# A two-layer encoder in split fp32: output operands get buffers of their own, casts go behind the probabilities' cast, first products are reordered, a product moves from GpSimd to VectorE

## The chip, the cores and the metric

The kernel runs on one core of a Trainium2 chip. The metric is the device time of one execution in microseconds (us); the figure for a kernel is the median of its runs. Engines are called TensorE (PE in the profile), VectorE (DVE), ScalarE (ACT), GpSimd (POOL) and SyncE (SP). Every engine works through its own instructions in one fixed order, and waits at an instruction until what that needs has been signalled by another engine or by a DMA. "L648" is line 648 of the kernel before.

## The reference

Two sequences (512 and 256 tokens, 768 in all, 2048 features, fp32) pass through two layers. Layer 0 projects x to an SSM branch (a_u, a_g) and to a grouped attention branch with 8 heads and 2 key/value heads (q, k, v, b_g); layer 1 is a dilated mixture attention with 16 heads and a gate. Cut to what matters here:

```python
# layer 0
a_u, a_g, q, k, v, b_g = split(x @ even_w_in)
ya = s5(a_u); ya = ya * sigmoid(ya @ glu_w + glu_b)           # the gated linear unit
q = rmsnorm(q) * qn_g; q = rotary(q, row | col); k likewise    # cosine and sine products
yb = softmax(q @ k.T * scale) @ v
y = concat(ya * silu(a_g), yb * silu(b_g)) @ even_w_out
x = layernorm(ALPHA * x + y) * ln_g + ln_b
# layer 1
q, k, v, g = split(x @ odd_w_in)
y = (dilated_mixture(rotary(q), rotary(k), v) * silu(g)) @ odd_w_out
out = layernorm(ALPHA * x + y) * ln_g + ln_b
```

## The kernel before, in words

Every fp32 operand of a matrix product is split into a high part (a cast on ScalarE, L441 or L447, names ending in h) and a low part (the difference, on VectorE or GpSimd, L442 or L448, names ending in l). A product is then three matmuls: high by high, high by low, low by high. Activations live in `c.xh` and `c.xl`, 16 blocks of 128 features by 768 tokens; weights are loaded by SyncE (`wr`, `b`) and split into `wh`, `wl`.

The order of the work is written out by hand as a recording. Long matmul loops (`proj_f`, L536, 128x384 products into `pa`/`pb`; `proj_t`, L580, products into `pt`; `Seven.product`, L753) call `fill(c)` after each group of products. `fill` takes a function from the queue `c.q` and runs what `later(c, n, f)` has put down for n fills from now. So small pieces (transposes, attention steps, norms) are placed between groups of long products. A scheduler then orders each engine's instructions; `tc.issue_after(x)` keeps an instruction behind x on its engine, and a tile pool gives out buffers, so a tile is only written once the readers of its buffer's last use are done.

Five places matter:

- **Query blocks** (`qk_block`, `q_block`, L635 to L675). Four blocks of queries, each in three parts i. A part is copied from PSUM, normalised (`qss`, `qn`: L660 to L663, with a power on GpSimd at L662), multiplied by a sine table (four products, `qsq`, L669, VectorE) and by a cosine table (two products 128x256, `qr`<-`qn`,`qkc`, L672, GpSimd), summed (L673, VectorE) and transposed on TensorE (`ps_q`, L648) after the number of fills in `at`. The keys go the same way. For the last block `at` is (1, 2, 3).
- **Attention of layer 0** (`Attn.step`). A step issues the scores of one unit of 128 queries (`ps_sc`, L843), turns the probabilities `pp` of the unit two steps earlier (`ps_pt`, L872, split into `pth` and `ptl` by `split_ps`), and, when a sequence is complete, the values (`ps_o`, L885). Steps stand in `c.q` between the products of the last gate (`late_gate(7)`) and of the gated linear unit (L1142 on, one fill per six products). One `fill(c, 2)` stands between these two (L1141).
- **First products of layer 1** (`Seven`). Layer 1's projections are done by seven products of sums of blocks in place of eight. For the first four weight pairs n, products 0 and 3 need no sums and are done alone (`Seven.alone`, L1302 on); ScalarE copies each result to `early` (L761). The sums of activations come from VectorE (L1208), ScalarE casts them (L1216), VectorE takes the low part.
- **Gates of layer 1** (`gate_sb`, L1437). The projections come back from DRAM into a `res` tile; ScalarE takes a tanh (L1439, 128x768), VectorE the product (L1440). This happens for two heads at a time, 16 heads in all.
- **First block of the output projection** (L1485 to L1505). While the last head pair's attention steps still run, the block of 256 output columns is started: `mix_in(k)` loads head k's mixed values from DRAM into a `res` tile (three buffers, shared with queries, keys and gates of the last heads), and splits it into `c.xh[k]`, `c.xl[k]`. It runs three blocks ahead of the products. `residual1` applies the norm's scale and offset to the residual `res0` in two passes on GpSimd (L1350, 128x1536), each with a row tile `lrow` fetched by GpSimd's queue.

## Time and profile before

| | us |
|---|---|
| median of 3 runs | 2634.8 (2634.49 to 2635.05) |
| the profiled execution's own time | 2632.97 |
| its span | 2631.2 |

| engine | busy, us | share of the span | instructions |
|---|---|---|---|
| TensorE (PE) | 2541.3 | 97% | 15632 |
| VectorE (DVE) | 1787.2 | 68% | 3516 |
| ScalarE (ACT) | 1050.0 | 40% | 2102 |
| GpSimd (POOL) | 772.5 | 29% | 641 |

About 1.8 us of the profiled execution lie around its span. The mean granted clock of TensorE is 0.986 of full speed. A view that lists waits names, for each instruction that stood idle, the engine and the tile that released it; a timeline row gives the start, the length, the engine, the line, the instruction with output and inputs, and in brackets the idle time before it. Long rows of equal products are grouped by "xN".

### The profile page before, as it was taken

Reading aid. Unit: us, or ns where it says so; the run is one execution under the profiler, and the core shown is the slowest. Engines: PE = TensorE matmul, PEld = TensorE weight load, DVE = VectorE, ACT = ScalarE, POOL = GpSimd, SP = SyncE. Lnnn points to the kernel's source line nnn. Section 1 sums busy time; section 2 is a strip of 40 time slices with the busy share of each in tenths; the row PEclk is TensorE's granted clock in tenths of the full one; section 3 lists DMA queues with packets and bytes.
Section 4 is the critical chain, followed back from the end, with each engine's and each line's share of the span. In section 5 each row is a group of like instructions: output and inputs, shape, how many; then the busy total and the mean of one; then the engine's idle time right before and its main releaser. Section 6 shows DMA issues by size and latency. Waiting matters only on the chain.

```text
span 2631.2 us, 41939 instructions
## 1 busy us (share of the span) xinstructions
PE 2541.3 (97%) x15632; PEld 2432.2 (92%) x15632; DVE 1787.2 (68%) x3516; ACT 1050.0 (40%) x2102; POOL 772.5 (29%) x641
## 2 busy tenths in 40 slices
PE   7999999999999999998999999999999999989996
PEld 7999999999988998888999999999999999988886
DVE  6488998878445542238866666778788878763437
ACT  4322233222237731117433333456555656651111
POOL 2555666645564420004000000012212212244404
PEclk9999999999999999999999999999999999989998
DMA  5433333332354462125443444454544454456222
GB/s 154 124 88 99 96 98 97 102 88 71 110 150 141 142 207 64 64 89 165 138 131 124 129 126 127 137 117 111 119 115 109 112 117 113 101 163 196 77 74 106
DMA packets 353451, 308.59 MB, mean 117 GB/s; under 512 B 60384, under 2 KB 305120, under 8 KB 352352
## 3 DMA queue, kind: packets, MB, share of 16 engines
q1 hardware_dynamic: 333200, 265.83, 33.3%
q0 software_dynamic: 10688, 36.71, 6.9%
q10 hardware_dynamic: 9360, 3.38, 0.7%
q8 instruction: 123, 2.02, 0.3%
q14 instruction: 80, 0.66, 0.1%
HBM read 232.10 MB, written 67.44 MB: 114 GB/s over the span
## 4 chain that ended last, share of the span: by engine, by line
PE 70%; DVE 16%; DMA 4%; issue 3%; POOL 2%; ACT 1%; SPq 0%; DVEq 0%; POOLq 0%; ACTq 0%
PE pt L580 23%; PE ps_y L753 12%; PE ps_z L753 8%; PE ps_x L753 8%; PE pa L536 4%; PE pb L536 4%; PE ps_o L885 3%; PE ps_sc L843 2%; DMA res<-pd 2%; PE ps_pt L872 2%; DVE wl L442 1%; DVE tmpv L227 1%; DVE xs L370 1%; PE ps_y L410 1%; DVE sc_sw L369 1%
## 5 line engine op out<-in xcount | busy, mean ns | idle before, releaser
L441 ACT CAST wh<-wr 128x512 fp32r<-128x512 f32 x348 | 216.3, 622 | 715.3 <-PE pt L580 391.5
L580 PE MATMUL pt<-wh,xh 128*128 128x256 f32 (+1 forms) x1392 | 458.8, 330 | 0.9 <-DVE z L898 0.8
L580 PE MATMUL pt<-wl,xh 128*128 128x256 f32 (+1 forms) x1392 | 456.1, 328 | 0.0
L580 PE MATMUL pt<-wh,xl 128*128 128x256 f32 (+1 forms) x1392 | 455.9, 327 | 0.0
L442 POOL TENSOR_TENSOR wl<-wr,wh 128x512 fp32r<-128x512 f32 x176 | 245.1, 1398 | 532.7 <-ACT wh L441 470.0
L442 DVE TENSOR_TENSOR wl<-wr,wh 128x512 fp32r<-128x512 f32 x172 | 145.8, 849 | 257.0 <-ACT wh L441 256.4
L580 PEld LDWEIGHTS pt<-wh,xh 128*128 128x128 f32 x1392 | 265.8, 191 | 25.0 <-issue 2.5
L580 PEld LDWEIGHTS pt<-wl,xh 128*128 128x128 f32 x1392 | 265.8, 191 | 22.3
L580 PEld LDWEIGHTS pt<-wh,xl 128*128 128x128 f32 x1392 | 265.5, 191 | 22.3
L753 PE MATMUL ps_y<-xh,wh 128*128 128x384 f32 x768 | 260.0, 339 | 0.0
L753 PE MATMUL ps_y<-xl,wh 128*128 128x384 f32 x768 | 257.1, 335 | 0.9 <-DVE xl L1208 0.9
L753 PE MATMUL ps_y<-xh,wl 128*128 128x384 f32 x768 | 257.0, 335 | 0.0
L441 ACT CAST wh<-b 128x512 fp32r<-128x512 f32 x248 | 151.6, 619 | 184.4 <-PE ps_z L753 91.5
L442 DVE TENSOR_TENSOR wl<-b,wh 128x512 fp32r<-128x512 f32 x248 | 170.2, 688 | 38.4 <-ACT wh L441 38.2
L753 PE MATMUL ps_x<-xh,wh 128*128 128x384 f32 x512 | 176.1, 344 | 7.5 <-ACT early L761 6.1
L753 PE MATMUL ps_z<-xh,wh 128*128 128x384 f32 x512 | 174.1, 340 | 0.0
L753 PE MATMUL ps_x<-xh,wl 128*128 128x384 f32 x512 | 172.0, 336 | 0.0
L753 PE MATMUL ps_x<-xl,wh 128*128 128x384 f32 x512 | 171.9, 336 | 0.0
L753 PE MATMUL ps_z<-xh,wl 128*128 128x384 f32 x512 | 171.4, 335 | 0.0
L753 PE MATMUL ps_z<-xl,wh 128*128 128x384 f32 x512 | 171.1, 334 | 0.0
L536 PE MATMUL pa<-xh,wh 128*128 128x384 f32 x448 | 158.3, 354 | 4.4 <-ACT xh L447 3.3
L536 PE MATMUL pa<-xh,wl 128*128 128x384 f32 x448 | 151.5, 338 | 0.6 <-POOL wl L442 0.4
(355 smaller groups left out, 6374.7 us busy)
## 6 DMA issues: line engine op xcount, KB each, us to landing
b<-in_odd_w_in_dram SPq DMA_DIRECT2D x256, 256.0 KB, 3.0
wr<-in_even_w_in_dram SPq DMA_DIRECT2D x144, 256.0 KB, 3.3
pd<-z SPq DMA_DIRECT2D x56, 384.0 KB, 2.5
wr<-in_even_w_out_dram SPq DMA_DIRECT2D x64, 256.0 KB, 2.6
wr<-in_odd_w_out_dram SPq DMA_DIRECT2D x64, 256.0 KB, 3.0
res<-pd POOLq DMA_DIRECT2D x16, 768.0 KB, 6.9
res<-pd POOLq DMA_DIRECT2D x16, 576.0 KB, 6.4
nd<-z POOLq DMA_DIRECT2D x12, 512.0 KB, 4.2
```

What stands on the lines that cost most here:

```text
L227: e.tensor_tensor(out=tmp, in0=pt(9 + j), in1=xt(sx), op=ALU.mult)
L369: v.tensor_tensor(out=sw, in0=sw, in1=bc(ai), op=ALU.mult)
L370: v.tensor_tensor(out=x1, in0=x1, in1=sw, op=ALU.add)
L410: nc.tensor.matmul(o, s.ca[:, 0, g, 1:9].rearrange("p j c -> p (j c)"), s.xs[:, 0:8, :, g].rearrange("p j r -> p r j"), start=False, stop= ...
L441: cast = nc.scalar.copy(hi, src)
L442: (eng or nc.gpsimd).tensor_tensor(out=lo, in0=src, in1=hi.bitcast(F32), op=ALU.subtract)
L536: nc.tensor.matmul(out[n][s][:, 0:HALF], wt[:, j], xt[k][:, HALF * s:HALF * s + HALF], start=k == k0 and i == 0, stop=k == nk - 1 and i == 2)
L580: nc.tensor.matmul(view[t], xt[k][:, tok], wt[:, j], start=first and i == 0 and ti % per == 0, stop=last and i == 2 and ends)
L753: nc.tensor.matmul(ps, w[:, k], x(k), start=i < 3 and k == j == 0, stop=k == 3 and j == 2, skip_group_check=i >= 3)
L843: nc.tensor.matmul(s, a[:, qs], b[:, ks], start=j == 0, stop=j == 2)
L872: nc.tensor.transpose(ps[:, 128 * j:128 * j + 128], seq.ps[i][:, 128 * j:128 * j + 128], c.ident)
L885: nc.tensor.matmul(o, a, b[:, j], start=j == 0 and x == 0, stop=j == nt - 1 and x == 2)
```

## The change

The diff has six edits:

- The cosine product of queries and keys (L672) runs on VectorE instead of GpSimd, and the last query block's transposes come one fill later each, at (2, 3, 4).
- The `fill(c, 2)` before the gated linear unit is gone, so its two attention steps come between the unit's products.
- `Seven.alone` runs product 0 of all four pairs, then product 3 of all four, instead of 0 and 3 pair by pair.
- `split_ps` returns its cast, `turn` keeps it in `att.cast`, and the tanh of `gate_sb` is held behind that cast. For the last gates the two tanh also come later (5 and 8 fills, not 4 and 5).
- Mixed values are loaded by `mix_load` into a pool of their own, `pm`, with five buffers, four blocks ahead; the first two go into one `res` tile. `mix_in` splits two blocks ahead, its cast held behind `att.cast`. More fills stand between the products, and the queue is emptied at block 4.
- `residual1` of the first block runs on VectorE, after the queue is emptied, and `res0` is loaded at block 9.

```diff
@@ split_ps
-    nc.scalar.copy(hi, src)
+    cast = nc.scalar.copy(hi, src)
     nc.vector.tensor_tensor(out=lo, in0=src, in1=hi.bitcast(F32), op=ALU.subtract)
+    return cast
@@ qk_block
-            nc.gpsimd.tensor_tensor(out=o, in0=u, in1=cg[:, 2 * i + tt].unsqueeze(1).to_broadcast([128, 2, 128]), op=ALU.mult)
+            nc.vector.tensor_tensor(out=o, in0=u, in1=cg[:, 2 * i + tt].unsqueeze(1).to_broadcast([128, 2, 128]), op=ALU.mult)
@@ Attn.turn
-        split_ps(nc, pv, *(t[:, :, 128 * at:128 * at + 128] for t in seq.pt))
+        self.cast = split_ps(nc, pv, *(t[:, :, 128 * at:128 * at + 128] for t in seq.pt)).ins
@@ layer 0
-            q_block(3, at=(1, 2, 3))
+            q_block(3, at=(2, 3, 4))
...
-            fill(c, 2)
             for f in range(8):
@@ layer 1, first products
-                for n in range(n_first):
-                    for i in (0, 3):
+                for i in (0, 3):
+                    for n in range(n_first):
                         sv.alone(n, i, lambda: fill(c, 2))
@@ residual1
-        def residual1(pool, z, x):
+        def residual1(pool, z, x, eng=nc.gpsimd):
...
-                nc.gpsimd.tensor_tensor(out=z, in0=z, in1=row.unsqueeze(1).to_broadcast([128, 6, 256]), op=op)
+                eng.tensor_tensor(out=z, in0=z, in1=row.unsqueeze(1).to_broadcast([128, 6, 256]), op=op)
@@ gates
-                        later(c, 4 + i, lambda i=i: gate_sb(blocks[i], two[i], i))
+                        later(c, 4 + i if n < 31 else 5 + 3 * i, lambda i=i: gate_sb(blocks[i], two[i], i))
...
-                nc.scalar.activation(out=g, in_=t, func=AF.Tanh, scale=0.5)
+                with tc.issue_after(att.cast):
+                    nc.scalar.activation(out=g, in_=t, func=AF.Tanh, scale=0.5)
@@ mixed values
+            mixed = {}
+
+            def mix_load(k, raw=None):
+                if k < 15:
+                    mixed[k] = pm.tile([128, TOK], F32, tag="mi", name="mi", bufs=5) if raw is None else raw
+                    nc.sync.dma_start(mixed[k], md[k])
+
             def mix_in(k):
                 if k < 15:
-                    raw = pc.tile([128, 4, HALF], F32, tag="res", name="res", bufs=3).rearrange("p a n -> p (a n)")[:, 0:TOK]
-                    nc.sync.dma_start(raw, md[k])
-                    split_sb(nc, raw, c.xh[k], c.xl[k], nc.vector)
+                    with tc.issue_after(att.cast):
+                        split_sb(nc, mixed[k], c.xh[k], c.xl[k], nc.vector)
@@ first output block
-            nc.sync.dma_start(res0, nd[:, :, 0:256])
-            residual1(pc, res0, 0)
...
-            for k in order1[:3]:
+            first = pc.tile([128, 4, HALF], F32, tag="res", name="res", bufs=3).rearrange("p a n -> p (a n)")
+            for k in order1[:2]:
+                mix_load(k, first[:, TOK * k:TOK * k + TOK])
                 mix_in(k)
+            for k in order1[2:4]:
+                mix_load(k)
 
             def each(k):
-                m = order1.index(k) + 3
-                if k in (1, 3, 9):
+                m = order1.index(k)
+                if k in (1, 3, 9, 11, 13):
                     fill(c)
-                if k == 10:
+                if m < 12:
+                    mix_load(order1[m + 4])
+                if m < 14:
+                    mix_in(order1[m + 2])
+                if k == 9:
+                    nc.sync.dma_start(res0, nd[:, :, 0:256])
+                if k == 4:
                     flush(c)
-                if m < 16:
-                    mix_in(order1[m])
+                    residual1(pm, res0, 0, nc.vector)
```

TensorE's instructions are the same in number and kind; their order differs at four places: the last query block, the start of the gated linear unit, the first products of layer 1 and the first output block. Three pieces of the other engines' order follow; behind each `L` stands the line in the kernel it is from.

ScalarE at the start of the gated linear unit, before (`kh`, `vh` <-`ld` are keys and values of the second half of the heads, `mx` is a finished head, `pp` the probabilities, `pth` their transposed high part):

```order
L441 CAST xh<-mx 128x512
L447 CAST pth_8973<-ps_pt 128x2x128
L848 ACTIVATE pp,sst<-ps_sc,sst 128x512
L441 CAST wh<-wr 128x512
L854 ACTIVATE pp<-pp,sst 128x512
L447 CAST pth_9049<-ps_pt 128x4x128
L848 ACTIVATE pp,sst<-ps_sc,sst 128x512
L441 CAST kh<-ld 128x768
L854 ACTIVATE pp<-pp,sst 128x512
L441 CAST xh<-mx 128x256
L447 CAST pth_9049<-ps_pt 128x4x128
L848 ACTIVATE pp,sst<-ps_sc,sst 128x512
```

and in the changed kernel:

```order
L441 CAST wh<-wr 128x512
L855 ACTIVATE pp<-pp,sst 128x512
L441 CAST kh<-ld 128x768
L441 CAST vh<-ld 128x768
L441 CAST xh<-mx 128x512
L447 CAST pth_8986<-ps_pt 128x2x128
L849 ACTIVATE pp,sst<-ps_sc,sst 128x512
L855 ACTIVATE pp<-pp,sst 128x512
L447 CAST pth_9067<-ps_pt 128x4x128
L849 ACTIVATE pp,sst<-ps_sc,sst 128x512
L441 CAST xh<-mx 128x256
```

The casts of keys and values have moved together and ahead of a cast of transposed probabilities; before, they stood steps apart (the cast of `vh` follows the last row of the first piece).

ScalarE among the first products of layer 1, before:

```order
L441 CAST wh<-wr 128x512
L1216 CAST xh<-z 128x4x128
L1192 ACTIVATE z<-ps_n,lbT,lgT 128x128 x3
L761 COPY early<-ps_x 128x384
L1216 CAST xh<-z 128x4x128
L1192 ACTIVATE z<-ps_n,lbT,lgT 128x128
L1216 CAST xh<-z 128x4x128 x3
L761 COPY early<-ps_x 128x384
L1216 CAST xh<-z 128x4x128
L761 COPY early<-ps_x 128x384
L1216 CAST xh<-z 128x4x128
L441 CAST wh<-bt 128x512
```

and in the changed kernel:

```order
L441 CAST wh<-wr 128x512
L762 COPY early<-ps_x 128x384
L1216 CAST xh<-z 128x4x128
L1192 ACTIVATE xh<-ps_n,lbT,lgT 128x128
L1192 ACTIVATE z<-ps_n,lbT,lgT 128x128 x3
L762 COPY early<-ps_x 128x384
L1216 CAST xh<-z 128x4x128
L1192 ACTIVATE z<-ps_n,lbT,lgT 128x128
L1216 CAST xh<-z 128x4x128
L441 CAST wh<-bt 128x512
L762 COPY early<-ps_x 128x384
```

Copies of the alone products have moved ahead of casts of the sums, which VectorE has to deliver.

VectorE at the start of the first output block, before (`ql`, `kl` are the low parts of the last head's queries and keys, `xl`<-`res` or `xl`<-`mi` those of mixed values):

```order
L442 TENSOR_TENSOR xl<-res,xh 128x768
L758 TENSOR_TENSOR res<-ps_y,res 128x384
L850 ISA pp,sst<-ps_sc,mixt 128x256
L850 ISA sst 128x1
L442 TENSOR_TENSOR ql<-res,qh 128x768
L853 RECIPROCAL sst<-sst 128x1
L448 TENSOR_TENSOR ptl<-ps_pt,pth 128x4x128
L442 TENSOR_TENSOR kl<-res,kh 128x768
L758 TENSOR_TENSOR res<-ps_z,res 128x384
L442 TENSOR_TENSOR xl<-res,xh 128x768
```

and in the changed kernel:

```order
L442 TENSOR_TENSOR ql<-res,qh 128x768
L854 RECIPROCAL sst<-sst 128x1
L448 TENSOR_TENSOR ptl<-ps_pt,pth 128x4x128
L442 TENSOR_TENSOR kl<-res,kh 128x768
L759 TENSOR_TENSOR res<-ps_z,res 128x384
L442 TENSOR_TENSOR xl<-res,xh 128x768
L759 TENSOR_TENSOR res<-ps_y,res 128x384
L442 TENSOR_TENSOR xl<-res,xh 128x768
L442 TENSOR_TENSOR xl<-mi,xh 128x768
L1350 TENSOR_TENSOR res_24634<-res_24634,lrow 128x1536
L851 ISA pp,sst<-ps_sc,mixt 128x512
```

The low part of the first mixed block has moved from ahead of `ql` to behind `kl`, and the residual's two passes (the first is the row before the last) are now in VectorE's row.

## Rows read from the trace of the kernel before

**Rows 1.** Waits of TensorE, whole span: total us, times, longest us.

```profile
PE ps_q L648 <- DVE qr L673: 10.9, 4, 5.7
PE ps_o L885 <- ACT pth L447: 7.1, 2, 5.3
PE ps_x L753 <- ACT early L761: 6.1, 3, 3.5
PE ps_pt L872 <- ACT pp L854: 4.9, 2, 3.7
```

**Rows 2.** Stretches: length, busy time per engine, granted clock, DMA share, GB/s.

```profile
749.00:768.00 19.00, 13.73 (x74) 12.81 (x73) 13.49 (x22) 5.33 (x9) 13.69 (x12) 0.92 0.34 97
790.00:806.00 16.00, 11.09 (x51) 9.60 (x50) 7.79 (x18) 10.73 (x25) 3.52 (x3) 0.79 0.48 159
1217.00:1240.00 23.00, 16.87 (x81) 15.92 (x81) 21.54 (x29) 15.18 (x32) 7.15 (x6) 0.85 0.53 160
2316.00:2361.00 45.00, 34.16 (x229) 32.30 (x228) 28.99 (x46) 26.82 (x51) 18.52 (x11) 0.85 0.59 176
```

**Rows 3.** Timeline of TensorE, queries' transposes: start, length, instruction, idle before.

```profile
649.56 0.66 PE L648 MATMUL ps_q<-ident,qr 128*128 128x128 f32 x2 [5.65 <-DVE qr L673]
752.07 0.66 PE L648 MATMUL ps_q<-ident,qr 128*128 128x128 f32 x4 [2.31 <-DVE qr L673]
757.70 0.66 PE L648 MATMUL ps_q<-ident,qr 128*128 128x128 f32 x4 [0.80 <-DVE qr L673]
```

**Rows 4.** Timeline of VectorE, first query block.

```profile
643.12 0.89 DVE L669 TENSOR_TENSOR qsq<-qn,qks 128x128 f32<-128x128 f32 x4
646.45 2.37 DVE L669 TENSOR_TENSOR qsq<-qn,qks 128x128 f32<-128x128 f32 x4
```

**Rows 5.** All instructions of line 672.

```profile
L672 POOL TENSOR_TENSOR qr<-qn,qkc x30: 723/788/1187, 620.5 to 760.1; 128x256 f32<-128x256 f32 x30
```

**Rows 6.** Timeline of TensorE before the gated linear unit.

```profile
797.69 1.11 PE L872 MATMUL ps_pt<-ident,pp 128*128 128x128 f32 x4 [3.72 <-ACT pp L854]
```

**Rows 7.** Timeline of TensorE, first products of layer 1.

```profile
1233.57 0.69 PE L753 MATMUL ps_x<-xh,wh 128*128 128x384 f32 x1 [3.50 <-ACT early L761]
```

**Rows 8.** Timeline of VectorE, the same stretch.

```profile
1234.15 1.28 DVE L1208 TENSOR_TENSOR xl<-z,xh 128x512 fp32r<-128x512 f32 x2
```

**Rows 9.** Timeline of TensorE, end of layer 1's attention.

```profile
2316.03 0.28 PE L580 MATMUL pt<-wh,xh 128*128 128x256 f32 x1
2321.90 0.80 PE L843 MATMUL ps_sc<-kl,qh 128*128 128x512 f32 x1 [3.32 <-DVE kl L442]
2336.84 0.58 PE L885 MATMUL ps_o<-pth,xh 128*128 128x256 f32 x1 [5.30 <-ACT pth L447]
```

**Rows 10.** Timeline of VectorE, the same stretch.

```profile
2314.83 5.48 DVE L442 TENSOR_TENSOR ql<-res,qh 128x768 fp32r<-128x768 f32 x1 [1.17 <-ACT qh L441]
2320.31 0.67 DVE L448 TENSOR_TENSOR ptl<-ps_pt,pth 128x512 fp32r<-128x512 f32 x1
2320.90 0.94 DVE L442 TENSOR_TENSOR kl<-res,kh 128x768 fp32r<-128x768 f32 x1
2321.76 0.55 DVE L758 TENSOR_TENSOR res<-ps_z,res 128x384 f32<-128x384 f32 x1
```

**Rows 11.** Timeline of GpSimd, the same stretch.

```profile
2313.47 2.56 POOL L442 TENSOR_TENSOR wl<-wr,wh 128x512 fp32r<-128x512 f32 x2
2315.97 3.52 POOL L1350 TENSOR_TENSOR res<-res,lrow 128x1536 f32<-128x1536 f32 x1
```

**Rows 12.** Timeline of ScalarE, the same stretch.

```profile
2316.28 0.84 ACT L441 CAST kh<-res 128x768 fp32r<-128x768 f32 x1 [0.51 <-DMA res<-rt]
2334.95 0.84 ACT L1439 ACTIVATE g<-res 128x768 f32<-128x768 f32 x1 [3.33 <-DMA res<-pd]
```

**Rows 13.** Row tiles of the norm: from issue to landing.

```profile
DMA to landing us min/median/max: 3.2/3.7/6.3
```

**Rows 14.** Waits of TensorE from 1750 to 2300 us.

```profile
PE ps_o L885 <- DVE ptl L448: 3.7, 4, 1.2
```

More of the change, by code (lines that the diff above doesn't have):

```diff
@@ L1488, in hybrid_kernel @@
             c.weng = nc.gpsimd
-            nc.sync.dma_start(res0, nd[:, :, 0:256])
-            residual1(pc, res0, 0)
+            mes = es.enter_context(ExitStack())
+            pm = mes.enter_context(tc.tile_pool(name="pm", bufs=1))
             order1 = [0, 1, 2, 3, 8, 9, 10, 11, 12, 13, 4, 5, 6, 7, 14, 15]
-            for k in order1[:3]:
+            first = pc.tile([128, 4, HALF], F32, tag="res", name="res", bufs=3).rearrange("p a n -> p (a n)")
+            for k in order1[:2]:
+                mix_load(k, first[:, TOK * k:TOK * k + TOK])
                 mix_in(k)
+            for k in order1[2:4]:
+                mix_load(k)
             def each(k):
-                m = order1.index(k) + 3
-                if k in (1, 3, 9):
+                m = order1.index(k)
+                if k in (1, 3, 9, 11, 13):
                     fill(c)
-                if k == 10:
+                if m < 12:
[5 more added lines that the diff above has]
+                if k == 4:
                     flush(c)
-                if m < 16:
-                    mix_in(order1[m])
+                    residual1(pm, res0, 0, nc.vector)
             _, view = proj_t(c, w_out1[0], *BLOCKS[0], order1, each=each)
             c.weng = nc.vector
+            mes.close()
         with rpool("pd") as pd:
```

## The prediction

> **What bounds the kernel now.** I read the list of TensorE's waits first, because TensorE is busy 97% of the span and its products are the same in number and kind before and after: time can only go where it stands idle, or runs slowly after having stood idle. The list [rows 1] names four groups at the places the change touches: query transposes waiting for VectorE's sum (10.9 us in 4 waits), values waiting for the probabilities' cast (7.1 in 2), first products waiting for ScalarE's copy (6.1 in 3), and transposes of probabilities (4.9 in 2). Then the table of stretches [rows 2]: at each place the granted clock lies under 1.00, so a wait costs more than its length. There are two levels, 1.2 and 2.4 GHz; a mean of 0.85 over the 45 us from 2316 on means that 30% of it, 13.5 us, ran at 1.2 GHz. Had all of those been busy, 6.7 us would be lost; some were idle time, so I take 4.5. In the same way 749 to 768 loses at most 1.5 (I take 1.2), 790 to 806 at most 3.4 (I take 2), 1217 to 1240 at most 3.4. Then the timelines of the engines that TensorE waits for, place by place.
>
> **Query blocks.** In the last block the three transposes wait 2.31, 0.80 and, as the remainder of the 10.9 us after these and the 5.65 of the first block, 2.16 us: 5.27 in all [rows 1, 3]. Between two of them stands one fill, 24 products: from the end of one row of transposes, 752.73, to 757.70 less 0.80 of waiting, some 4.2 us. Each transpose now comes one fill later, and 4.2 is more than the longest of the three waits. The two cosine products on VectorE must fit as well. Thirty products of 0.79 us leave GpSimd [rows 5]; VectorE has no such row, but four of its 128x128 products took 0.89 us in one place and 2.37 in another, the second beside GpSimd's work [rows 4], so a 128x256 product is bounded by 0.4 and 1.2 us. Two of them at 0.4 replace two at 0.79. All 5.27 us go, with 1.2 of slow clock. The first block keeps its place, and its wait of 5.65 shortens only by what VectorE's chain gains. Without GpSimd's products beside them the four sine products need 0.89 rather than 2.37, which is 1.5 off, and two products of 0.4 are put in front, 0.8 on: 0.7, and with a little clock 0.9 (bounds -1.2, where both products take 1.2 and the sine products only get to 1.2 less, and 1.6). Query blocks: 5.27 + 1.2 + 0.9 = 7.4.
>
> **Start of the gated linear unit.** Two steps stood in a row with nothing between them, and the second waited 3.72 us [rows 6], both together 4.9 [rows 1]. Now six products, about 1 us, stand ahead of each, and ScalarE and VectorE need less catching up; with the waits the slow clock's 2 us go. Against it stands ScalarE's order: the casts of keys and values have moved together and in front of a cast of probabilities, and the second of them needs its load to have landed. A load that ScalarE had to wait for elsewhere cost it 3.33 us [rows 12]. So the new wait is between 0 and 3.3, and I take 1.9, as some products cover it: 4.9 + 2 - 1.9 = 5.0.
>
> **First products of layer 1.** Three waits of 6.1 us, the longest 3.50 [rows 7], are for a copy that stands in ScalarE's row behind casts of sums which VectorE has to deliver. With four product 0s in a row the copies stand ahead of those casts, and TensorE arrives up to 6.1 us earlier at the next products, which need VectorE's low parts. But VectorE is busy 21.54 of these 23 us [rows 2], and the two low parts for them end at 1235.4 [rows 8], after the last copy. VectorE's work is no less than before. So the wait changes its owner, from ScalarE to VectorE; I give 1.5 us of gain, from work moved ahead, with bounds 0 and 6.1 + 3.4.
>
> **Gates of layer 1.** From 1750 to 2300 us values wait four times for a low part, 3.7 us in all [rows 14], each time just behind a pair of tanh. With the tanh behind the probabilities' cast that cast is early, but VectorE still takes the masked scores of the same step first, so only the gate's product goes from in front: a third, 1.2 (bounds 0 and 3.7).
>
> **First output block.** Two waits here are for ScalarE: 5.30 [rows 9], and the remainder of 7.1 [rows 1], 1.8. In the first ScalarE was itself held by a tanh that waited 3.33 us for its tile's load [rows 12]; the cast of probabilities stood behind it. In the other a mixed block's cast, waiting for its load, stood in front. Loads into own buffers start as much as four blocks ahead, and both kinds now stand behind the cast: 7.1 goes. The first wait, 3.32, is another case. The low part `ql` took 5.48 us, not the 0.94 of the equally long `kl` [rows 10], and ended 0.8 us after GpSimd's pass over the residual did (2315.97 + 3.52) [rows 11]. That pass has left GpSimd, so `ql` can run when GpSimd's weight splits end at 2316.03: it ends at 2317.0, `ptl` at 2317.6, `kl` at 2318.6 (its cast ends at 2317.1 [rows 12]). But the first mixed block's low part now stands behind `kl`, with a 0.55 us sum between: it ends at 2320.1. TensorE is ready for it at 2316.03 [rows 9] plus four products that need only the cast, 0.15 each (34.16 us for 229 [rows 2]): 2316.6. So 3.5 us of waiting take the place of 3.32. The residual's second pass waits for a row tile, 3.2 to 6.3 us after its issue [rows 13], and a unit's masked scores stand behind it on VectorE; by then TensorE has more than two blocks to do, so I count 0.6 (bounds 0 and 4). Of the 4.5 us of slow clock half stays with the new wait. Sum: 7.1 + 3.3 - 3.5 - 0.6 + 2.3 = 8.6, and 0.4 for a small wait that follows the 5.30: 9.0.
>
> The Trainium skill, "SBUF — State Buffer", section "SBUF: two separate sides", states that VectorE with two SBUF inputs and GpSimd share a port pair as an exclusive lock: whichever starts first keeps it for the whole instruction. The trace agrees with that at `ql`: 5.48 us beside 3.52 of GpSimd, and not a slower rate of both. By that rule each of the thirty moved products may wait for a weight split of GpSimd's, 1.28 us apiece here [rows 11]; the first query block would then lose its 0.9 and up to 1.2 more.
>
> **Sum.** 7.4 + 5.0 + 1.5 + 1.2 + 9.0 = 24.1. Against the profiled execution's own 2632.97 that is 2608.9; the median of the runs shown, 2634.8, is 1.8 higher, so I forecast 2610.7, say 2611.
>
> **Rivals.**
> *VectorE takes over more of the waits.* It gets thirty products and two residual passes and is the busy engine at three of the places. Then the first query block loses 1.2 instead of gaining 0.9, first products and gates gain nothing, the scores behind the residual come 4 us late instead of 0.6, and the new wait at the linear unit is 3.3: 24.1 - 2.1 - 2.7 - 3.4 - 1.4 = 14.5, or 2620. For it: 21.54 of 23 us. Against it: elsewhere VectorE has a third of its time free.
> *The waits go and nothing replaces them.* First products gain their 6.1 + 2, and the first mixed block finds its low part early enough: 24.1 + 6.6 + 3.5 + 2.2 = 36.4, or 2598. Against it speak the two rows of VectorE's order that I counted.
> *A new wait behind the tanh makes it slower.* The tanh of each pair of gates stands behind the cast, but in front of the exponentials of the next unit; it waits for a load (3.33 us in the row shown), and there are 8 pairs. If TensorE came to wait for what stands behind it, over 3 us at each of the 8 pairs would use up the whole 24 and the kernel would be slower, at 4 us by 8: 2643. The point from which it decides is 3 us a pair. Against it: the tanh waits for the same load in the kernel before, with more behind it.
>
> **Chances and range.** The forecast has 0.62, VectorE's rival 0.20, the full gain 0.13, the tanh 0.05. About 0.2%, 5.3 us, is what a measurement can tell from no change. The first three cases are faster by more; of VectorE's I leave 0.02 within it and 0.01 beyond, so: faster 0.92, same 0.03, slower 0.05. The range, 2601 to 2623, takes in VectorE's rival and the likelier part of the full gain.
>
> **What would show it.** Right: the three transposes of the last query block without idle time; a wait of 3 to 4 us before the first output products' third group with `xl` as releaser, and none of 5 us behind a tanh; first products released by `xl` on VectorE, not by `early`. Wrong: waits of TensorE for `pth` or `pp` at every pair of gates; a wait for `qr` that has grown; masked scores 3 us late behind the residual's second pass; or a sum of waits at these five places above 15 us.

## The result, and the profile after

| | before | after |
|---|---|---|
| median of 4 runs each, us | 2634.64 (2631.41 to 2635.05) | 2604.67 (2601.58 to 2610.26) |
| the profiled execution's own time, us | 2632.97 | 2603.28 |
| its span, us | 2631.2 | 2601.5 |
| VectorE busy, us | 1787.2 | 1775.3 |
| GpSimd busy, us | 772.5 | 744.8 |

The changed kernel takes 0.9891 of the time before, with a 95% interval of 0.9872 to 0.9911. The two spans differ by 29.7 us. Lines from L449 to L1140 are one higher than before, and so are the tanh and the gate's product (now L1440, L1441); L441 to L448, L1208, L1216 and L1350 stand where they stood.

The waits of TensorE at the changed places come first again (total us, times, longest us). Of the four rows of before [rows 1] one is left, halved; one is a fifth; two are gone. The two waits for a cast `xh` are new. The values waited for `ptl` before as well, 5.4 us in six waits, and the last row had 0.9.

```profile
PE ps_y L754 <- ACT xh L1216: 7.4, 1, 7.4
PE ps_q L649 <- DVE qr L674: 5.5, 2, 3.3
PE pt L581 <- ACT xh L441: 4.1, 1, 4.1
PE ps_o L886 <- DVE ptl L448: 3.0, 1, 3.0
PE ps_pt L873 <- ACT pp L855: 1.0, 1, 1.0
PE ps_y L754 <- DVE xl L1208: 0.7, 1, 0.7
```

The stretches of the same places, shifted to where the work now lies (length, busy time of TensorE, its weight loads, VectorE, ScalarE and GpSimd, granted clock, DMA share, GB/s). Against [rows 2] the clock is 1.00 at the gated linear unit and 0.96 at the first output block, and still 0.91 and 0.90 at the last query block and the first products (first and third row; the third covers 35 us here and 23 in [rows 2]).

```profile
745.00:764.00 19.00, 15.68 (x89) 15.32 (x88) 15.02 (x28) 6.64 (x12) 9.90 (x7) 0.91 0.40 118
785.00:801.00 16.00, 14.96 (x89) 13.57 (x88) 8.21 (x20) 13.78 (x31) 9.37 (x6) 1.00 0.58 184
1195.00:1230.00 35.00, 26.94 (x154) 26.23 (x153) 32.05 (x47) 22.54 (x52) 12.22 (x12) 0.90 0.60 180
2295.00:2340.00 45.00, 37.45 (x288) 36.04 (x287) 34.87 (x50) 31.25 (x61) 13.69 (x10) 0.96 0.60 172
```

Waits alone don't give the gain, since the granted clock was lower around the long ones (0.79 from 790 to 806 us before, where 1.00 stands now). So I took the start of each TensorE instruction in the trace before, subtracted the start of the one with the same number in the other trace, and read by how much this lead grows over a stretch at whose two ends both kernels have done the same. In us of lead gained (stretches in the time of before):

| place | forecast | after | after, second trace |
|---|---|---|---|
| first 450 us, which the change doesn't touch | 0 | 1.6 | -1.8 |
| first query block, 635 to 700 | 0.9 | 3.2 | 4.3 |
| last query block, 700 to 777 | 6.5 | 1.3 | 2.6 |
| start of the gated linear unit, 780 to 840 | 5.0 | 6.8 | 6.3 |
| the rest of the unit, 840 to 960 | 0 | 2.3 | 2.4 |
| first products, 1190 to 1260 | 1.5 | 0.3 | -0.4 |
| gates, 1745 to 2295 | 1.2 | 5.0 | 3.1 |
| first output block, 2296 to 2380 | 9.0 | 7.1 | 5.9 |
| 2380 to 2500 | 0 | 1.7 | about the same |

The second column of the changed kernel is a profiled execution of a later run of it. The two differ by up to 2 us at a place, and the traces of all kernels below show that this is too narrow: where their edit leaves a place alone, the gates gain from 1.7 to 6.7 us and the first output block from 4.3 to 7.1. The first 450 us, where every instruction is the same as before, lay between -5.5 and 4.9 us. Loads that land differently there are a likely reason, but this was not tried. It is why whole times of single kernels differ by more than most edits under test, and why the experiments are read by place. The intervals of two experiments alone, the two fills and the tanh, lie clear of the changed kernel's 0.9872 to 0.9911.

### The profile page after: what moved, and what is told of

It reads as the page before. It is cut to its first block, busy times and chain, and to the rows that moved or that the text cites. A ratio compares the mean times of both kernels' runs of the same rounds, so it can differ in the third digit from the quotient of the medians.

```text
span 2601.5 us, 41922 instructions
## 1 busy us (share of the span) xinstructions
PE 2530.4 (97%) x15632; PEld 2428.0 (93%) x15632; DVE 1775.3 (68%) x3548; ACT 1050.8 (40%) x2102; POOL 744.8 (29%) x609
## 4 chain that ended last, share of the span: by engine, by line
PE 78%; DVE 12%; issue 4%; POOL 3%; DMA 2%; ACT 1%; DVEq 0%; SPq 0%; POOLq 0%; ACTq 0%
PE pt L581 24%; PE ps_y L754 14%; PE ps_z L754 9%; PE ps_x L754 9%; PE pa L537 5%; PE pb L537 5%; PE ps_o L886 3%; PE ps_sc L844 3%; PE ps_pt L873 2%; POOL wl L442 1%; DVE wl L442 1%; PE ps_y L410 1%; PE ps_s L300 1%; DVE tmpv L227 1%; DVE xs L370 1%
## 5 line engine op out<-in xcount | busy, mean ns | idle before, releaser
L441 ACT CAST wh<-wr 128x512 fp32r<-128x512 f32 x348 | 216.0, 622 | 727.0 <-PE pt L581 370.1
L442 DVE TENSOR_TENSOR wl<-wr,wh 128x512 fp32r<-128x512 f32 x172 | 136.7, 796 | 259.8 <-ACT wh L441 259.4
L1407 POOL DMA_DIRECT2D rt<-res x64 | 32.9, 514 | 714.5 <-DMA cos<-in_c_rope_dram 472.9
L441 ACT CAST wh<-b 128x512 fp32r<-128x512 f32 x248 | 151.5, 620 | 202.5 <-PE ps_z L754 105.6
```

Of the source, the lines that this page charges most:

```text
L441: cast = nc.scalar.copy(hi, src)
L442: (eng or nc.gpsimd).tensor_tensor(out=lo, in0=src, in1=hi.bitcast(F32), op=ALU.subtract)
L1407: nc.gpsimd.dma_start(rt[32 * i:32 * i + 32], t[0:32, i])
```

## The experiments

The times are medians, with the ratio to the kernel before on the same chip and its 95% interval. Each experiment edits the changed kernel.

**The cosine products back on GpSimd.**

```diff
-            nc.vector.tensor_tensor(out=o, in0=u, in1=cg[...], op=ALU.mult)
+            nc.gpsimd.tensor_tensor(out=o, in0=u, in1=cg[...], op=ALU.mult)
```

> The changed kernel with one line undone: the cosine products of line 672 run on GpSimd again; the later fills (2, 3, 4) stay. Theory (VectorE's sine products were slow because GpSimd's products held its port): the wait of the first query block, 2.19 us in the changed kernel, grows back to between 5 and 6 us, some 3.2 us with the slow clock, and the places behind 780 us stay as in the changed kernel. Rival (the first block's gain comes from elsewhere, such as the slower or faster start of the run): the wait stays near 2.2 us. For the last query block the later fills alone should remove the first two of its three waits in both theories; the third, 3.32 us in the changed kernel, shows whether the moved products made it.

2609.01 us, ratio 0.9918 (0.9895 to 0.9941). The first query block loses its gain (-1.3 where the changed kernel has 3.2), and the wait of [rows 3] is back there:

```profile
654.98 0.87 PE L649 MATMUL ps_q<-ident,qr 128*128 128x128 f32 x3 [5.61 <-DVE qr L674]
```

But the last block gains 5.7 instead of 1.3. The moved products are worth 4.5 us at one place and cost 4.4 at the other.

**GpSimd for the last block alone.** `q_block(3, at=(2, 3, 4), eng=nc.gpsimd)`, VectorE for the other blocks and the keys.

> The changed kernel with the cosine products on VectorE for all blocks but the last query block, where they run on GpSimd. From u1_mult_gpsimd (first block 1.27 us slower than before, last block 5.73 faster) against the changed kernel (3.21 and 1.33 faster), theory: the two places are independent, and this kernel keeps the 3.2 us of the first and has the 5.7 of the last, 4.4 us faster than the changed kernel, with no wait for qr after 745 us. Rival (the last block's third wait depends on when GpSimd's weight splits fall, not on the products): it stays at 1.3 to 3 us for the last block.

2605.23 us, 0.9895 (0.9842 to 0.9947). Both halves come: 2.9 at the first block, 5.7 at the last. The last transpose's wait falls from 3.32 to the first row here. Most of the time won is spent at once: the start of the linear unit gains 3.5 instead of 6.8, for TensorE now comes to it before ScalarE's probabilities are ready (second row). Last block and linear unit together gain 11.5 us, where kernels with VectorE's products there gain 10.1 to 11.5, so nothing clear is saved.

```profile
762.70 0.66 PE L649 MATMUL ps_q<-ident,qr 128*128 128x128 f32 x4 [1.49 <-DVE qr L674]
786.09 0.38 PE L844 MATMUL ps_sc<-kh,qh 128*128 128x256 f32 x1 [1.32 <-ACT pp L849]
```

**The two fills in a row again.**

```diff
+            fill(c, 2)
             for f in range(8):
```

> The changed kernel with the fill of two steps ahead of the gated linear unit put back. From 780 to 960 us the changed kernel gains 9.1 us, 6.2 of them by 830 us. Theory: all of it is from the two steps that now have products between them, so 9 us are lost again, with a wait of 3 to 4 us for pp near 790 us, and the wait for ptl at the unit's end near 920 us comes back, since the attention ends two fills earlier. Rival (the unit gains from the query block's later transposes as well): only about 6 us are lost and the end near 920 us stays without a wait.

2612.01 us, 0.9950 (0.9928 to 0.9973). Two waits return, at the start of the unit and 137 us later; the two stretches gain 1.8 and 0.0 instead of 6.8 and 2.3.

```profile
788.52 0.66 PE L873 MATMUL ps_pt<-ident,pp 128*128 128x128 f32 x4 [3.71 <-ACT pp L855]
925.56 0.39 PE L886 MATMUL ps_o<-ptl,vh 128*128 128x256 f32 x1 [1.28 <-DVE ptl L448]
```

**First products pair by pair again.**

```diff
-                for i in (0, 3):
-                    for n in range(n_first):
+                for n in range(n_first):
+                    for i in (0, 3):
```

> The changed kernel with the first products of layer 1 in pairs again (product 0, then 3, pair by pair). Theory (VectorE's sums bound this stretch, and the order only moves the wait from ScalarE's copy to ScalarE's cast of a sum): the stretch from 1190 to 1255 us takes as long as in the changed kernel, within 0.6 us, with three waits for early in place of one of 7.4 us for xh. Rival (the row of four products 0 gains): 1.5 us or more are lost.

2602.19 us, 0.9902 (0.9865 to 0.9939). The place gains 1.1 against 0.3 and -0.4 for the new order, so the new order gains nothing that these traces can tell. TensorE's waits from 1190 to 1240 us are those of before again [rows 1, 7]:

```profile
PE ps_x L754 <- ACT early L762: 6.1, 3, 3.5
PE ps_y L754 <- DVE xl L1208: 0.9, 1, 0.9
```

**The first products' weight splits on VectorE.** `c.weng = nc.vector` in place of `nc.gpsimd` for `alone`. If VectorE's sums were late because of GpSimd's passes beside them, the 7.36 us should shrink.

> The changed kernel with the weights' low parts of the eight alone products of layer 1 on VectorE instead of GpSimd. VectorE bounds the stretch from 1190 to 1230 us. Theory (a two-input operation of VectorE stands still while GpSimd works on two inputs): each of GpSimd's splits of 1.3 to 1.8 us costs VectorE 1.1 us of standing still, some 5 in the stretch, against 0.6 us for each split that VectorE takes over, so the wait of 7.36 us for xh shrinks by 1 to 3 us. Rival (the two only share, or VectorE is just busy): eight more operations of 0.6 us make the wait longer by 2 to 5 us.

2606.02 us, 0.9898 (0.9843 to 0.9952). The place gains 0.8, within the spread of the changed kernel's two traces. The waits fall from 8.1 to 6.4 but move to the weights. Inconclusive.

```profile
PE ps_y L754 <- ACT wh L441: 4.4, 1, 4.4
PE ps_y L754 <- DVE xl L1208: 2.0, 1, 2.0
```

**The tanh not held behind the probabilities' cast.**

```diff
-                with tc.issue_after(att.cast):
-                    nc.scalar.activation(out=g, in_=t, func=AF.Tanh, scale=0.5)
+                nc.scalar.activation(out=g, in_=t, func=AF.Tanh, scale=0.5)
```

> The changed kernel with the tanh of the gates no longer held behind the probabilities' cast; all else stays. From 1750 to 2290 us the changed kernel gains 5.0 us on the kernel before, where I had forecast 1.2. Theory (the tanh that waits for its load kept the weights' cast and the probabilities' cast behind it): 4 to 5.5 us are lost again in that stretch, with waits of TensorE for ptl at the pairs of gates, 3 to 4 us in all. Rival (the gain comes from loads that land at other times, as everything comes 15 us earlier): under 1.5 us are lost.

2614.49 us, 0.9947 (0.9921 to 0.9972). From 1745 to 2295 us this loses 4.5 us to before, where the changed kernel gains 5.0 and every other kernel with the hold at least 1.7. That is more than the 4 to 5.5 expected, and why the stretch falls behind the kernel before is open. Six waits stand there that the changed kernel does not have, 6.9 us in all:

```profile
PE ps_o L886 <- DVE ptl L448: 4.6, 4, 1.2
PE ps_o L886 <- ACT pth L447: 2.3, 2, 1.3
```

ScalarE's row shortly ahead of one of them, which came at 1840.5:

```profile
1838.09 1.58 ACT L1439 ACTIVATE g<-res 128x768 f32<-128x768 f32 x2 [5.68 <-DMA res<-pd]
```

**Two buffers for the norm's row in the first output block.** `lrow` gets `bufs=2` there, so that its second fetch need not wait for the first pass.

> The changed kernel with two buffers for the row tile of the first block's residual, so that both rows are fetched early. In the changed kernel TensorE waits 3.00 us for ptl, which stands on VectorE behind masked scores and these behind the residual's second pass, which waits 3.20 us for its row. Theory (the row's fetch is the cause): that wait goes, and the stretch from 2296 to 2380 us is 3 to 4 us shorter than in the changed kernel. Rival (VectorE's two passes of 1.75 us are too much work there, wherever the row is): a wait of 1.5 us or more for ptl or pp remains.

2604.39 us, 0.9891 (0.9834 to 0.9949). The 3.0 us for `ptl` is gone, but the other wait grew from 4.1 to 5.9, and the place gains 7.9 for 7.1: no difference. The second fetch now stands in GpSimd's queue ahead of the write-back of the last queries and keys, and that takes 9.0 us to land instead of 7.9.

```profile
PE pt L581 <- ACT xh L441: 5.9, 1, 5.9
```

**The first two mixed blocks' casts not held.** `mix_in(k, False)` for them.

> The changed kernel with the casts of the first two mixed blocks not held behind the probabilities' cast; the later ones stay held. In the changed kernel TensorE waits 4.09 us for the cast of the first block and 0.46 us for its low part, both behind the last head's queries and keys. Theory (the order put them there): these 4.5 us go, but the next wait is the one for the last head's low parts, as the rotated queries land late (ScalarE stood 4.87 us for them): 1.5 to 3 us are gained in all. Rival (the landing of the rotated queries alone decides, whatever the order): under 1 us is gained. A third outcome: 4 us or more, if TensorE has enough to do with the first blocks.

2602.45 us, 0.9884 (0.9832 to 0.9936). The waits from 2290 to 2330 us fall from 7.6 to 5.6, and the first now stands at the last keys, which are late too. The place gains 7.6, hardly more than the spread: taken by itself, the order of the casts is not what holds TensorE there.

```profile
PE ps_o L886 <- DVE ptl L448: 3.2, 1, 3.2
PE ps_sc L844 <- ACT kh L441: 1.8, 1, 1.8
PE ps_sc L844 <- DVE kl L442: 0.6, 1, 0.6
```

**Three buffers for mixed values instead of five, the residual loaded at block 12.** Fewer bytes ahead of the write-back.

> The changed kernel with three buffers for mixed values instead of five (so at most three loads run ahead) and the load of the residual asked for at block 12 instead of 9. In the changed kernel five loads of 384 KB and one of 768 KB are issued in the same 2 us as the write-back of the last head's rotated queries and keys (four transfers of 48 KB), and these take 7.9 us to land, against 1.8 us in the kernel before; ScalarE stands 4.87 us for them with the mixed blocks' casts behind. Theory (the burst of loads is the cause of the first wait): the write-back lands in 3 to 5 us, and the wait of 4.1 us for xh before the first output products falls to 2 us or less. Rival (the order alone, casts behind queries and keys, is the cause): the write-back may land sooner, but the wait stays at 3 us or more.

2604.82 us, 0.9909 (0.9888 to 0.9930). The write-back landed in 7.5 us instead of 7.9, the wait stayed 4.0, the place gains 5.7. A miss: with three loads beside it the write-back is about as late as with five. What stands ahead of it in GpSimd's own queue, the fetch of the norm's row, was the same in both.

**The loads behind the write-back.** Mixed values, except the first two blocks, and the residual are issued by GpSimd, in whose queue the write-back stands ahead of all but one of them.

```diff
-                    nc.sync.dma_start(mixed[k], md[k])
+                    (nc.sync if raw is not None else nc.gpsimd).dma_start(mixed[k], md[k])
...
-                    nc.sync.dma_start(res0, nd[:, :, 0:256])
+                    nc.gpsimd.dma_start(res0, nd[:, :, 0:256])
```

> The changed kernel with the loads of mixed values (all but the first two) and of the residual issued from GpSimd's queue instead of SyncE's. There the write-back of the last head's rotated queries and keys stands ahead of all of them but one load of 384 KB, so the burst of five loads and the residual can no longer be in front of it; nothing else of the order is touched on purpose, and the mixed blocks' first casts stay behind those of queries and keys. d4_loads_few, with three loads ahead, left the landing at 7.5 us and the wait for xh at 4.05 us. Theory (the write-back shares the DMA engines with what was issued before it, so the burst decides): it lands in under 4.5 us and the wait for xh falls to 1.5 us or less. Rival (the order of the casts makes the wait, whenever the write-back lands): the landing gets shorter, but the wait stays above 2.5 us. Third outcome: the landing stays at 7 us, and then neither the number nor the place of these loads makes it.

2600.21 us, 0.9891 (0.9847 to 0.9936). The write-back lands in 2.7 us (DMA issues from 2280 to 2300 us: number, KB each, median us to landing):

```profile
res<-rt POOLq DMA_DIRECT2D x4, 48.0 KB, 2.7
```

and of the wait for the first blocks 0.9 is left, with the norm's 3.1:

```profile
PE ps_o L886 <- DVE ptl L448: 3.1, 1, 3.1
PE pt L581 <- DVE xl L442: 0.9, 1, 0.9
```

The place gains 12.3, 5.2 more than in the changed kernel. So a write-back that lands early removes that wait. What made it late is not settled, because the edit moved two things. In the changed kernel the fetch of the norm's row stands directly ahead of the write-back in GpSimd's queue (first two rows); here it is issued far behind it (third row):

```profile
2286.66 0.57 POOL L1349 DMA_DIRECT2D lrow<-in_ln_g_dram  x1 [5.83 <-DVE sst L854]
2287.22 1.99 POOL L1418 DMA_DIRECT2D res<-rt  x4
2301.39 0.55 POOL L1349 DMA_DIRECT2D lrow<-in_ln_g_dram  x1
```

Either the burst of loads or this fetch, which itself takes 6.2 us, can have held the write-back. For the fetch speak the experiment with three loads (7.5 us) and the one with two fetches ahead (9.0 us). In the changed kernel the write-back's packets begin 5.1 us after its issue, at 2292.27, just as the fetch's packets end (2292.51). In the experiment with the first casts not held they begin 1.2 us after the fetch's have ended, so the fetch alone does not explain all. A run that moves only the fetch was not made.

**Four edits together.** GpSimd for the last block's cosine products, two row buffers, first casts not held, three buffers; beside it on the same chip the changed kernel again.

> The changed kernel with four edits that the runs before point to: three buffers for mixed values, the first two casts not held, both row tiles of the residual fetched at once, and the last query block's cosine products on GpSimd. By place, from the runs: last query block 3 to 4 us less, of which the linear unit may take back 2 or 3; first output block 2 to 4 us less. Theory: 3 to 6 us faster than the changed kernel, so a ratio to the kernel before of 0.987 to 0.988. Rival (the places give back what they gain, as each gain lets later loads meet in time): within 2 us of the changed kernel.

> The changed kernel itself, on the same chip as the run that combines the four edits, for their comparison: 28 us by place without the first 450 us of the program, in which loads land differently in each execution; a ratio to the kernel before of about 0.989.

2596.26 us, 0.9873 (0.9856 to 0.9890), against 2606.39 us, 0.9911 (0.9894 to 0.9928): 10 us less than the changed kernel. By place about 6 us of it can be seen, nearly all in the first output block, which gains 12.1 for 5.9; in their traces 5.4 more lie in the first 450 us, where both do the same. Its waits from 2285 to 2330 us are 2.8 in all, for the last keys (`kh` 2.3, `kl` 0.5).

The write-back landed in 6.7 us there. So the block gains as much with a late write-back, when the first casts don't stand behind it and both rows of the norm are fetched early; each of these edits alone gained little. Putting the loads behind the write-back as well was not tried.

## Why the prediction was right, and where its steps failed

2604.7 lies inside the range of 2601 to 2623, 6.3 us under the forecast of 2611, nearer to the 2598 of the rival in which nothing replaces the waits than to the 2620 of VectorE's. The sum of 24.1 stands against 29.7 by the first trace and 24.5 by the second, on whose chip the medians differ by 22.9. That it comes so near is partly luck: the forecast was 4 to 5 us too high at the last query block and 2 to 3 too high at the first output block, 4 too low at the linear unit, and 2 to 4 too low at the gates and at the first query block.

The mechanism held less well than the number. Of the signs named for being right, the first products were indeed no longer released by `early`, and no wait of 5 us stood behind a tanh; but the third transpose of the last query block waits, and at the first products and the first output products the main wait is for a cast, not for `xl`. Of the signs for being wrong three came: a wait for `qr` grew (3.32, where that block had at most 2.31), masked scores stood some 3 us behind the residual's second pass, and the rows of waits above add up to 21.7 us, over the 15 that were named. That last bound was badly set, as the prediction's own terms leave some 19 us of waits.

**Query blocks: 7.4 forecast, 4.5 and 6.9 measured, of these 1.3 and 2.6 at the last block where 6.5 was forecast. The step that failed is "All 5.27 us go".** Two of the three transposes of the last block wait no more; the third waits longer than any of the three did:

```profile
761.67 1.09 PE L649 MATMUL ps_q<-ident,qr 128*128 128x128 f32 x4 [3.32 <-DVE qr L674]
```

Two things were wrong. "4.2 is more than the longest of the three waits" compares one fill with one wait, but a later fill is won once, and the waits add up: of 5.27 some 1.1 had to stay, and 1.49 stayed with the cosine products on GpSimd. The other 1.8 came with the moved products, for which I took 0.4 us each. VectorE's chain ahead of that wait:

```profile
755.55 3.52 DVE L670 TENSOR_TENSOR qsq<-qn,qks 128x128 f32<-128x128 f32 x4
758.99 1.81 DVE L673 TENSOR_TENSOR qr<-qn,qkc 128x256 f32<-128x256 f32 x2
760.84 0.69 DVE L674 TENSOR_TENSOR qr<-qr,qsq 128x512 f32<-128x512 f32 x1
```

GpSimd's beside it:

```profile
754.92 2.29 POOL L442 TENSOR_TENSOR ql<-ld,qh 128x768 fp32r<-128x768 f32 x1
757.18 1.34 POOL L442 TENSOR_TENSOR wl<-wr,wh 128x512 fp32r<-128x512 f32 x1
```

The four sine products end soon after GpSimd's splits end at 758.52; four such took 0.89 us in [rows 4]. The Trainium skill, "SBUF — State Buffer", section "SBUF: two separate sides", has these passes exclude each other whole; these rows fit that. But slow sine products were not new at this place. In before they took nearly as long, beside GpSimd's cosine products and splits, in a row that the prediction did not read:

```profile
759.27 3.08 DVE L669 TENSOR_TENSOR qsq<-qn,qks 128x128 f32<-128x128 f32 x4
```

From the first sine product to the end of the sum VectorE took 5.3 us before and takes 6.0 now. The normalisation ahead of them (L663, now L664), which fell on a weight split of GpSimd's, took 1.77 instead of 0.69. These two make up the 1.8. With GpSimd's own products in that queue (the first two experiments) the last block gains 5.7, near the 6.5 forecast. At the first block the sign was right and the size too small: 3.2 to 4.3 for 0.9, because the wait of 5.65 fell to 2.19 rather than by 0.7. The 5.7 that the experiment won at the last block was half returned at the linear unit in one trace, so the error cost the sum little.

**Gated linear unit: 5.0 forecast, 9.1 and 8.7 measured.** The mechanism was right, the new wait was mis-sized: 1.0 for 1.9, and the clock is 1.00 at once. 2.3 more came behind 840 us. About half of it is a row that I had not read: the stretch's last values waited in before, too. The experiment with the two fills, which gains nothing there, shows that the whole of it belongs to the same edit.

```profile
935.43 0.39 PE L885 MATMUL ps_o<-ptl,vh 128*128 128x256 f32 x1 [1.26 <-DVE ptl L448]
```

**First products: 1.5 forecast, 0.3 and -0.4 measured.** The wait changed its owner, as forecast, but to a cast on ScalarE (7.36), and only 0.7 to VectorE's low part. The cast starts at 1220.21; VectorE's sum just before it ends at 1219.23 + 0.68. In before the three waits were 6.1 and 0.9 more followed; now it is 8.1 in two. TensorE reaches the products of sums earlier and waits there for the same work: the lower bound, 0, was the answer. What would make the sums earlier is open.

**Gates: 1.2 forecast, 5.0 and 3.1 measured. The step that failed is "VectorE still takes the masked scores of the same step first".** VectorE and ScalarE of before, at one pair of gates:

```profile
1931.25 0.96 DVE L1440 SCALAR_TENSOR_TENSOR g<-g,res 128x768 f32<-128x768 f32 x1 [4.96 <-ACT g L1439]
1933.19 0.69 DVE L850 CUSTOM_DVE_ANT_0 pp<-ps_sc,mixt 128x512 f32<-128x512 f32 x1
1933.80 0.42 DVE L448 TENSOR_TENSOR ptl<-ps_pt,pth 128x256 fp32r<-128x256 f32 x1
```

```profile
1930.32 1.58 ACT L1439 ACTIVATE g<-res 128x768 f32<-128x768 f32 x2 [4.75 <-DMA res<-pd]
1932.32 0.36 ACT L447 CAST pth<-ps_pt 128x256 fp32r<-128x256 f32 x1
```

The masked scores (L850) were late because VectorE stood 4.96 us at the gate's product for a tanh that stood 4.75 for its load. They are not work that remains; they were queued behind the same stall. VectorE after has them and the low part done before the gate's product begins to wait:

```profile
1912.47 0.68 DVE L851 CUSTOM_DVE_ANT_0 pp<-ps_sc,mixt 128x512 f32<-128x512 f32 x1
1913.08 0.42 DVE L448 TENSOR_TENSOR ptl<-ps_pt,pth 128x256 fp32r<-128x256 f32 x1
1916.07 0.96 DVE L1441 SCALAR_TENSOR_TENSOR g<-g,res 128x768 f32<-128x768 f32 x1 [2.57 <-ACT g L1440]
```

So the 3.7 us go [rows 14] (0.4 is left in the second trace). The granted clock was 1.00 around these waits, 1925 to 1945 us for one, so none of the gain is the clock's; what the first trace has over 3.7 is within the spread. The experiment without the hold shows that the hold does it.

**First output block: 9.0 forecast, 7.1 and 5.9 measured.** The new wait was forecast at 3.5, for a low part on VectorE; 4.1 came for ScalarE's cast, and 0.5 for the low part. The size was nearly right, the reason wrong. ScalarE after stood still for the queries that its cast takes:

```profile
2295.57 0.83 ACT L441 CAST qh<-res 128x768 fp32r<-128x768 f32 x1 [4.87 <-DMA res<-rt]
```

These had been rotated and written back by four DMAs, and these are all DMAs of the changed kernel issued from 2286 to 2297 us (number, KB each, median us to landing):

```profile
mi<-md SPq DMA_DIRECT2D x5, 384.0 KB, 7.3
res<-nd SPq DMA_DIRECT2D x1, 768.0 KB, 10.8
wr<-in_odd_w_out_dram SPq DMA_DIRECT2D x2, 256.0 KB, 9.4
res<-rt POOLq DMA_DIRECT2D x4, 48.0 KB, 7.9
lrow<-in_ln_g_dram POOLq DMA_DIRECT2D x1, 128.0 KB, 6.2
```

In before the same four, from 2308 to 2318 us, with one load of 768 KB issued 3.9 us ahead of them and no row fetch in their queue (that one had been issued at 1700 us):

```profile
res<-rt POOLq DMA_DIRECT2D x4, 48.0 KB, 1.8
```

The prediction counted the early loads only as a gain; what stands beside them on the DMA engines, and that the row's fetch now comes ahead of the write-back, was left out. The Trainium skill, "DMA: Bandwidth & Descriptors", section "Issuing engines are not separate DMA queues", says that DMAs of all engines run on the same 16 DMA engines and interleave. The 7.9 us agree with that. The experiment that puts loads and fetch behind the write-back (2.7 us, 5.2 us of gain) shows that the late landing makes the wait, not which of the two makes it late. The second error is the residual's second pass, for which I took 0.6 out of 0 to 4: the values waited 3.0, and the experiment with two buffers for the row shows that its fetch is the cause.

```profile
2312.28 1.76 DVE L1350 TENSOR_TENSOR res<-res,lrow 128x1536 f32<-128x1536 f32 x1 [3.20 <-DMA lrow<-in_ln_b_dram]
2313.95 0.68 DVE L851 CUSTOM_DVE_ANT_0 pp<-ps_sc,mixt 128x512 f32<-128x512 f32 x1
```

No run undoes this block's own edits, so what each is worth is read from the traces alone. As forecast, `ql` takes 0.96 us instead of 5.48, with no pass of GpSimd beside it, and the waits of 5.30 behind the tanh and 3.32 for `kl` are gone.

**The rest.** 1.7 us from 2380 to 2500 us were in no term; every trace of a changed kernel gains them. There TensorE's products are the same in both kernels, and it waits 0.8 us for VectorE's `z` in before and not at all after. In before VectorE's weight split (first row) fell on a pass of GpSimd (second row), and in the changed kernel such a split took 0.69 us. This is read from the traces and was not tried by itself.

```profile
2441.26 3.45 DVE L442 TENSOR_TENSOR wl<-wr,wh 128x512 fp32r<-128x512 f32 x1 [3.39 <-ACT wh L441]
```

```profile
2440.66 3.50 POOL L1350 TENSOR_TENSOR z<-z,lrow 128x1536 f32<-128x1536 f32 x1 [3.28 <-DMA lrow<-in_ln_g_dram]
```

Of the rivals, VectorE's came true in two of its terms: the first products gained nothing, and the scores behind the residual came 3 us late. At the last query block, where that rival had named no price, VectorE took over a wait as well. A new wait behind the tanh came nowhere.

## What to carry to other kernels

When an instruction that waits for a load is moved back in its engine's row, count everything that stood behind it, on that engine and on the engines that wait for it: here a stall of 5 us at a gate had also delayed work that looked independent of it. When loads are moved forward, list the small transfers that then run beside them; four of 48 KB went from 1.8 to 7.9 us, and TensorE waited 4 us for what they carried. Look at their own queue, too, where another fetch had moved ahead of them. A piece of work that is moved one group of products later wins that group's time once, so compare it with the sum of the waits it is to cover, not with the longest. Price a short product on VectorE by the longest pass that GpSimd runs at the same moment, and judge an edit at its own place, since a wait removed is often met again at the next one.

## What the runs showed of the hardware

The stand-still of VectorE beside GpSimd is not general. In before, two operations of VectorE with one operand in PSUM took 0.74 us in the midst of a pass of GpSimd's that ran from 2448.51 for 3.50 us, while operations with two operands from SBUF took 3.45 (above), 5.48 [rows 10], and 3.84 us in the changed kernel (`xl<-mi`, beside 2.87 us of GpSimd's splits):

```profile
2449.90 0.74 DVE L898 SCALAR_TENSOR_TENSOR z<-z,pt 128x256 f32<-128x256 f32 x2
```

The four DMAs of 48 KB landed in 7.9 us behind a row fetch in their own queue and beside five loads of 384 KB and one of 768 KB of another engine's; in 7.5 us behind the same fetch and beside three of 384 KB; in 9.0 us behind two such fetches; and in 2.7 us with the fetch and all but one load behind them. In before it was 1.8 us. How much of this is the fetch's and how much the loads' was not separated.
